# Operand tiles moved to other SBUF bytes, zero-padded scores in block 1, and a PSUM tile copied out by ScalarE where MLA begins

## The chip, the cores and the metric

The kernel runs on one core of a Trainium2 chip. The metric is device time of one execution in microseconds. Three executions of the kernel before took 2668.88, 2670.66 and 2673.24 us (median 2670.66).

## The reference

Two model blocks on 512 tokens of width 1024, all in fp32. Activations are kept transposed (features on partitions, tokens along the free axis).

- **Block 1** puts 16 meta tokens in front (528 columns), then: `h += 0.5*swiglu(rmsnorm(h))` (FFN1, d_ff 2816); a mixer in which sliding-window attention (16 query heads of 64, 4 key heads, sink logits) and an S5 state-space branch are gated and merged through `w_out`; `h += 0.5*swiglu(rmsnorm(h))` again (FFN2, 512 columns), and a final rmsnorm with gain `final_norm`.
- **Block 2** has two layers. Layer 0 mixes with MLA: queries from a rank-512 and keys and values from a rank-256 projection, each with an rms norm, a 64-wide rotary part beside a 128-wide plain part, 16 heads, causal by chunks of 64. Layer 1 mixes with gated linear attention (GLA). After each mixer come layer norm, a conv FFN (`w_up`, a 3-tap conv, gelu gate, `w_down`), layer norm and a gated embedding `x + sigmoid(x W_g + b) * (p W_p)`.

## The kernel before, in words

**Matmuls.** Nearly all products are made by `mm3` (line 173) out of three matmuls of float32r operands: a weight `w` is split into `whi + wlo`, an activation into a high and a low tile (`zh`/`zl`, `mh`/`ml`, `oqh`/`oql` and so on), and `wh*zh`, `wh*zl`, `wl*zh` are summed in one PSUM bank. The stationary operand is a 128x128 piece of the weight, the moving operand the activation tile: 512 columns (`CS`, or `C512`, which is columns 16 to 528 of a 528-column tile), or two pieces of 264 columns (`C528`) where the meta tokens take part. `nat` (line 189) does the same with the activation stationary. Other products (scores, transposes, values, state-space) use plain f32 operands, for which each matmul shows as two in the trace.

**Weights** come by `fetch`: SP issues a 512 KB DMA into `raw`, ScalarE copies it to `whi`, VectorE subtracts for `wlo`.

**Order.** The program is written stage by stage, and a scheduler that simulates a timeline orders each engine's instructions; `issue_after`, `behind` and `chain` hold single instructions back. [...]

**SBUF.** Pools are laid one behind the other and given back in reverse; in a pool, tiles lie in the order of their first use. Of each partition 16384 bytes are reserved at the start (`dynamic_dma_scratch_size` at its default), then 128 bytes of constants, `cp` (21600 bytes), `wp` with the weights (49152), `sm` (960), and `zp` from byte 88224, which is 160 mod 512. `zp` holds `zh0, zl0, zh1, ...`, each in a slot of 2112 bytes (528 columns), so each of the 16 tiles begins 64 bytes later mod 512 than the one before: 160, 224, 288, ... Later stages use the first 512 columns of the same slots. The other operand tiles of 512 columns (2048 bytes) all begin at 416 mod 512 (`yh`, `gh` in pool `m3`; `ov`, `kh` in `a2`; `pth`, `mh`, `ml` in the conv FFNs), at 448 (`oqh`, behind the 16-byte tile `ovr`), or at 480 (`mh`, `ml` of FFN2, pool `f2`). All 128-column pieces of `whi` and `wlo` begin at 224 mod 512.

**Block 1's scores** (`scores1`, line 719): two key heads lie in one 128-row tile `kw`, head `s_` on rows `64*s_` on. For each of 4 query tiles two matmuls of 64 rows are issued, one for each half, into two banks of tag `q` (3 banks), each drained by VectorE with the mask (line 721). There are 8 units (`pp`, `n`) of 4 pairs, and 272 columns of keys (144 for `n == 0`). Between them stand the state-space quarters, queries and gates.

**MLA's beginning**: `project(0)` makes the two plain query products (`pn`) and the rotary product (`pr`) in PSUM, then the norm factor `Rq` of the query tokens (`spread_rsqrt`, into tile `oqR`); `sinT` and `cosT` are multiplied by `Rq` (line 1158, two instructions), and `queries` multiplies `pn` by `Rq` (`qn`) and lets `rotate` (lines 1086 to 1092) read `pr` from PSUM five times on VectorE. Behind the last rotation (`issue_after(last["rot"])`, lines 1238 to 1240) VectorE scales the eight residual tiles `hr` in place. `banks(...)` on line 1241 then deals the eight PSUM banks out anew, and a loop over 64 (head, query block) units follows; `project(1)` is its first filler, its first product in the bank that held `pr`.

Of the kernel before, what the change touches and what calls it, by code (L numbers as in the profile page):

```python
# [53 lines left out]
def body(nc, tc, A, out, es):  # L54
    cp = es.enter_context(tc.tile_pool(name="cp", bufs=1))
    wp = es.enter_context(tc.tile_pool(name="wp", bufs=2))
    sm = es.enter_context(tc.tile_pool(name="sm", bufs=2))
    zp = es.enter_context(tc.tile_pool(name="zp", bufs=1))
    psp = {}
# [47 lines left out]

    woff = {}


# [107 lines left out]
    def split_scaled(src, g, k, n):  # L218
        zh = zp.tile([P, n], F32R, name=f"zh{k}")
        zl = zp.tile([P, n], F32R, name=f"zl{k}")  # L220
        act(zh, src, AF.Copy, scale=g)
        stt(zl, src, g, zh.bitcast(F32), ALU.mult, ALU.subtract)
        return zh, zl

    def sumsq(tiles):
        acc = zp.tile([P, T1], F32, name="acc")
        n = tiles[0].shape[1]
        for k, t in enumerate(tiles):
            if k == 0:
                act(acc[:, :n], t, AF.Square)  # L230
            else:
                sq = zp.tile([P, T1], F32, name="sq", bufs=2)
                act(sq[:, :n], t, AF.Square)
                add(acc[:, :n], acc[:, :n], sq[:, :n], None if k == len(tiles) - 1 else GP)
        return acc[:, :n]
# [28 lines left out]

    def token_rsqrt(acc, scale, eps, R=None):

        pst = token_sums(acc)
        r = rsqrt(pst, pst.shape[1], scale, eps)
        if R is None:
            R = zp.tile([P, T1], F32, name="R")[:, :acc.shape[1]]  # L270
        spread_rsqrt(r, R)
        return r, R
# [353 lines left out]
    hold["dve"] = last["rsqrt"]  # L626
    R = zp.tile([P, T1], F32, name="R")
    hold["act"] = behind(lambda: spread_rsqrt(r, R))
# [19 lines left out]
    with tc.tile_pool(name="m1", bufs=1) as mp:  # L648
        att = mp.tile([P, 8, S], F32, name="att")
        with tc.tile_pool(name="m2", bufs=1) as ap_:  # L650
            for i4 in range(4):
                p = proj(wload("w_in", 1024), P, 0, z, C528)
                uf = ap_.tile([P, 4, MC], F32, name="uf", tag="sc", bufs=3)
                for i in range(2):
                    mul(uf[:, :, i * 66:(i + 1) * 66], p[:, i, :264].rearrange("p (m j) -> p j m", j=4),
                        R[:, i * 264:(i + 1) * 264].rearrange("p (m j) -> p j m", j=4))
                nc.sync.dma_start(u_d[i4 * P:(i4 + 1) * P], uf.rearrange("p j m -> p (j m)"))
            kw = []
            for mo in range(2):
                p = proj(wload("w_in", 1024), P, 0, z, C528)  # L660
                f = ap_.tile([P, T1], F32, name="kf", tag=f"sq{mo}")
                mul(v2(f), p[:, :, :264], v2(R))
                g = ap_.tile([P, 3, 272], F32, name=f"kw{mo}")
                GP.tensor_copy(g[:, 0], f[:, :272])
                for n in range(1, 3):
                    GP.tensor_copy(g[:, n, 0:NM], f[:, 0:NM])
                    GP.tensor_copy(g[:, n, NM:], f[:, NM + n * P:NM + (n + 2) * P])
                kw.append(g)
            banks(b=2, q=3, t=2, o=1)
# [36 lines left out]
            def scores1(u):  # L706
# [7 lines left out]
                for i in range(4):  # L714
                    pq = [pss("q"), pss("q")]
                    for s_ in range(2):
                        r = slice(64 * s_, 64 * s_ + 64)
                        kk = kw[pp][r, max(n - 1, 0), :W]
                        last["sc"] = PE.matmul(pq[s_][:, :W], qf[pp * 4 + i][r, n * P:(n + 1) * P], kk)  # L719
                    for s_ in range(2):  # L720
                        V.tensor_tensor_reduce(sc[s_][:, i, :W], pq[s_][:, :W], mk, 1.0, -3.0e38,
                                               ALU.add, ALU.max, st[s_][0][:, i:i + 1])
# [54 lines left out]
            for ui in range(len(units) + 1):  # L777
# [4 lines left out]
                if ui < 4:  # L782
                    query()
                elif 5 <= ui < 8:
                    gate(zp.tile([P, T1], F32, name="acc" if ui == 5 else "sq", bufs=1 if ui == 5 else 2)[:, :S])
                elif ui == 8:
                    with tc.issue_after(last["sc"].ins):
                        for i in range(2):
                            gate(mp.tile([P, S], F32, name=f"q{i}"))
# [77 lines left out]
    class Norm:  # L867


        def __init__(self, pool, xs, a):  # L870
            self.p, self.xs, self.a = pool, xs, a
            self.aq = zp.tile([P, T1], F32, name="acc")[:, :S]
            self.ad = pool.tile([P, S], F32, name="ad", bufs=1)

        def centre(self):

            pc = pss("s")
            PE.matmul(pc, oness, self.xs[0])
            self.c = zp.tile([P, T1], F32, name="R")[:, :S]
            act(self.c, pc, AF.Copy)  # L880
# [194 lines left out]
    with tc.tile_pool(name="a2", bufs=2) as mp:  # L1075
# [38 lines left out]
        r, _ = token_rsqrt(sumsq(ckv), 1.0 / 256, 1e-5, Rkv)  # L1114
        rkv = mp.tile([P, 4], F32, name="ovr", bufs=1)
        V.tensor_copy(rkv, r)
# [12 lines left out]

        def queries(d, pn, pr):  # L1130
            d["q"], d["r"] = [], []
            for p in pn:
                t = mp.tile([P, S], F32, name="qn", bufs=4)
                mul(t, p, Rq)
                d["q"].append(t)
                yield
            for p in pr:
                qr = mp.tile([P, S], F32, name="qr", bufs=1)
                q2 = mp.tile([P, S], F32, name="q2", bufs=1)
                rotate(qr, q2, p)  # L1140
# [8 lines left out]
        def project(pr_):  # L1149

            d = pair[pr_] = {}
            if pr_ == 0:
                pn = list(nope())
                pst = behind(lambda: token_sums(acc))
                pr = behind(lambda: list(rope()))
                r = rsqrt(pst, 4, 1.0 / 512, 1e-5)
                behind(lambda: spread_rsqrt(r, Rq))
                sc = mul(sinT, sinT, Rq), mul(cosT, cosT, Rq)
            yield from queries(d, pn if pr_ == 0 else nope(), pr if pr_ == 0 else rope())
            w = wload("w_ukv", 1024)  # L1160
# [76 lines left out]
        take([project(0)], 99)  # L1237
        with tc.issue_after(last["rot"].ins):
            for k in range(KD):
                stt(hr[k], hr[k], vcol("final_norm", k), R, ALU.mult, ALU.mult)  # L1240
        banks(b=2, q=2, t=2, o=1, s=1)
# [3 lines left out]
        for i in range(nu + 2):  # L1245
            if i < nu:
# [309 lines left out]
```

## Time and profile before

| | us |
|---|---|
| median of three executions | 2670.66 |
| the profiled execution | 2667.79 |
| its span, first to last instruction | 2666.0 |
| PE busy | 2620.0 (98%) |
| VectorE busy | 1590.7 (60%) |
| ScalarE busy | 959.7 (36%) |
| GpSimd busy | 227.7 (9%) |
| mean granted TensorE clock | 0.991 |

PE is TensorE's matmuls, PEld its weight loads, DVE VectorE, ACT ScalarE, POOL GpSimd. [...]

### The profile page before, as it was taken

The page shows a single profiled execution, that of the slowest core. Times are in us where ns is not written, and L with a number is a line of the kernel's source. Part 1 is how long each engine was busy: PE and PEld are TensorE (multiplying, and loading weights), DVE is VectorE, ACT ScalarE, POOL GpSimd, SP SyncE. Part 2 cuts the span into 40 slices and gives each one's busy share as a digit, 9 for nine tenths or more (in the row PEclk, how much of TensorE's full clock was granted, in tenths as well). Part 3 has the DMA queues.
Part 4 walks back from the last instruction along what each step waited for, and adds up shares of the span by engine and source line. Part 5 has one row for each costly group of instructions (what it writes and reads, how often), then busy time and mean ns, then how long its engine had stood idle before and what let it go on. Part 6 is the DMA issues. An engine that isn't in the chain of part 4 may idle for free.

```text
span 2666.0 us, 35024 instructions
## 1 busy us (share of the span) xinstructions
PE 2620.0 (98%) x13918; PEld 2186.8 (82%) x13918; DVE 1590.7 (60%) x2794; ACT 959.7 (36%) x1483; POOL 227.7 (9%) x186
## 2 busy tenths in 40 slices
PE   8999999899999999999999999999999999999999
PEld 8999999655888888887888878888778777888887
DVE  7985444685556544468766775555663356655556
ACT  4222223243333222234544454333353234433333
POOL 1000001231000000010000110000200011100020
PEclk9999999999999999999999999999999999999999
DMA  5443233331333333322112223333232221433331
GB/s 176 128 131 112 88 95 122 100 91 52 102 95 92 97 99 96 95 91 68 52 56 60 71 79 103 95 95 95 79 98 61 75 72 58 124 95 95 95 90 68
DMA packets 87748, 243.31 MB, mean 91 GB/s; under 512 B 20081, under 2 KB 26097, under 8 KB 87458
## 3 DMA queue, kind: packets, MB, share of 16 engines
q1 hardware_dynamic: 87586, 241.08, 29.3%
q8 instruction: 110, 1.80, 0.3%
q14 instruction: 52, 0.43, 0.0%
HBM read 229.11 MB, written 11.93 MB: 90 GB/s over the span
## 4 chain that ended last, share of the span: by engine, by line
PE 94%; DVE 3%; issue 1%; ACT 1%; DMA 0%; POOL 0%; SPq 0%; DVEq 0%; POOLq 0%; ACTq 0%
PE ps_b L173 63%; PE mm L173 16%; PE ps_b L189 6%; PE ps_o L1228 1%; PE ps_q L1200 1%; PE ps_o L1365 1%; PE ps_t L1216 1%; PE ps_o L772 1%; PE ps_u L1354 1%; PE ps_q L719 1%; PE ps_t L756 0%; DVE h L64 0%; DVE sq L64 0%; DVE wlo L64 0%; PE ps_q L1198 0%
## 5 line engine op out<-in xcount | busy, mean ns | idle before, releaser
L84 ACT ACTIVATE whi<-raw 128x1024 fp32r<-128x1024 f32 (+2 forms) x418 | 432.2, 1036 | 1050.1 <-PE ps_b L173 701.5
L64 DVE TENSOR_TENSOR wlo<-raw,whi 128x1024 fp32r<-128x1024 f32 (+2 forms) x418 | 516.5, 1238 | 341.2 <-ACT whi L84 337.9
L173 PE MATMUL ps_b<-zh,whi 128*128 128x512 f32 (+1 forms) x1656 | 653.1, 395 | 6.5 <-ACT zh L84 2.3
L173 PE MATMUL ps_b<-zh,wlo 128*128 128x512 f32 (+1 forms) x1656 | 654.7, 396 | 0.0
L173 PE MATMUL ps_b<-zl,whi 128*128 128x512 f32 (+1 forms) x1656 | 642.3, 391 | 0.0
L173 PEld LDWEIGHTS ps_b<-zh,whi 128*128 128x128 f32 (+1 forms) x1656 | 310.8, 188 | 82.6 <-issue 4.6
L173 PEld LDWEIGHTS ps_b<-zl,whi 128*128 128x128 f32 (+1 forms) x1656 | 311.3, 188 | 78.3 <-issue 2.6
L173 PEld LDWEIGHTS ps_b<-zh,wlo 128*128 128x128 f32 (+1 forms) x1656 | 310.7, 188 | 69.2
L173 PE MATMUL ps_b<-mh,wlo 128*128 128x512 f32 x528 | 208.5, 395 | 0.0
L173 PE MATMUL ps_b<-ml,whi 128*128 128x512 f32 x528 | 207.7, 393 | 0.0
L173 PE MATMUL ps_b<-mh,whi 128*128 128x512 f32 x528 | 207.6, 393 | 0.0
L173 PE MATMUL mm<-zh,whi 128*128 128x264 f32 x800 | 165.1, 288 | 6.2 <-ACT whi L84 5.8
L173 PE MATMUL mm<-zl,whi 128*128 128x264 f32 x800 | 164.2, 287 | 0.8 <-DVE zl L81 0.8
L173 PE MATMUL mm<-zh,wlo 128*128 128x264 f32 x800 | 164.1, 287 | 0.6 <-DVE wlo L64 0.6
L81 DVE SCALAR_TENSOR_TENSOR cv<-ps_b,vec,cv 128x511 f32<-128x511 f32 (+1 forms) x176 | 130.4, 745 | 16.0 <-ACT cv L84 14.5
L64 DVE TENSOR_TENSOR h<-h,ps_b 128x512 f32<-128x512 f32 x109 | 74.7, 686 | 104.6 <-PE ps_b L173 100.9
L173 PEld LDWEIGHTS mm<-zh,whi 128*128 128x128 f32 x800 | 126.1, 191 | 6.6 <-ACT whi L84 5.8
L173 PEld LDWEIGHTS mm<-zl,whi 128*128 128x128 f32 x800 | 125.2, 191 | 1.5 <-DVE zl L81 1.5
L173 PEld LDWEIGHTS mm<-zh,wlo 128*128 128x128 f32 x800 | 125.6, 190 | 0.8 <-DVE wlo L64 0.8
L64 POOL TENSOR_TENSOR acc<-acc,sq 128x512 f32<-128x512 f32 (+1 forms) x26 | 38.7, 1489 | 948.3 <-ACT sq L84 909.6
L173 PEld LDWEIGHTS ps_b<-mh,whi 128*128 128x128 f32 x528 | 99.2, 188 | 23.2 <-issue 0.5
L173 PEld LDWEIGHTS ps_b<-mh,wlo 128*128 128x128 f32 x528 | 99.2, 188 | 23.1 <-issue 0.5
(421 smaller groups left out, 4001.0 us busy)
## 6 DMA issues: line engine op xcount, KB each, us to landing
raw<-in_ffn_w_dram SPq DMA_DIRECT2D x130, 512.0 KB, 3.5
raw<-in_w_up_dram SPq DMA_DIRECT2D x88, 512.0 KB, 3.6
raw<-in_w_down_dram SPq DMA_DIRECT2D x44, 512.0 KB, 3.6
raw<-in_w_in_dram SPq DMA_DIRECT2D x32, 512.0 KB, 3.5
raw<-in_mla_o_dram SPq DMA_DIRECT2D x16, 512.0 KB, 3.6
raw<-in_ple_g_dram SPq DMA_DIRECT2D x16, 512.0 KB, 3.6
raw<-in_glu_dram SPq DMA_DIRECT2D x8, 512.0 KB, 3.5
raw<-in_w_out_dram SPq DMA_DIRECT2D x8, 512.0 KB, 3.5
```

What stands on the lines that cost most here:

```text
L64: return (e or V).tensor_tensor(o, a, b, op=op)
L81: return V.scalar_tensor_tensor(o, a, s, b, op0=op0, op1=op1)
L84: return SC.activation(o, a, f, **kw)
L173: last["pe"] = PE.matmul(o[:, i, :c1 - c0], lhs, x[k][r][:, c0:c1], start=(k == 0 and j == 0), stop=(k == kt - 1 and j == 2))
L189: PE.matmul(o[:m, :n], x[k][a][:, t0:t0 + m], w[b][:, kk_ * c + m0:kk_ * c + m0 + n], start=(k == 0 and i == 0), stop=(k == kt - 1 and i = ...
L719: last["sc"] = PE.matmul(pq[s_][:, :W], qf[pp * 4 + i][r, n * P:(n + 1) * P], kk)
L772: PE.matmul(po[64 * s_:64 * s_ + 64], vb[n - 1 + j][:, kv * 64:kv * 64 + 64], pT[s_][:, j], start=False, stop=(j == 1))
L1200: PE.matmul(p[:, :N], d["q"][e][:, bs], d["k"][e][:, :N], start=False, stop=True)
L1216: PE.transpose(pt[:, kt * P:(kt + 1) * P], sc[:, kt * P:(kt + 1) * P], ident)
L1228: PE.matmul(po[:, b * P:(b + 1) * P], vt[:, kt, e * P:(e + 1) * P], pT[:, kt * P:(kt + 1) * P], start=(kt == 0), stop=(kt == b))
L1354: PE.matmul(pu[c][:, :256], ek[b][rows, hc], vt[hh][rows, b])
L1365: PE.matmul(po[hh][-1][64 * c:64 * c + 64, (b % 2) * 256:(b % 2) * 256 + 256], qt[hh][:, n * 64:(n + 1) * 64], s_)
```

## The change: what it does

Four things, all on one core and with the same arithmetic:

1. **Bytes.** The reserved region shrinks from 16384 to 2048 bytes (14336 = 28 x 512 less). `zp` gets a 256-byte tile `gap` ahead and slots of 2560 bytes (`zw` = 640 columns), so every `zh`/`zl` of FFN1 and block 1 begins at 160 + 256 = 416 mod 512, and its column 16 at 480. Before `rp` the pool is closed and another, `zq`, opened in its place with a 320-byte `gap`: from FFN2 on every `zh`/`zl` begins at 160 + 320 = 480 mod 512, and, its 20 tiles being of 2048 bytes, so do the pools laid behind it (`a2`, the conv FFNs', GLA's). Gaps of 320 bytes in `m3` and 448 in `rt` put `yh`, `gh` and FFN2's `mh` at 480, and `rkv` takes 512 bytes in place of 16, which puts `oqh` at 480.
2. **Scores of block 1.** Each key head has tiles of its own, `kz[mo][e]`, 128 rows of which the other head's 64 are set to zero by GpSimd; the score matmuls take all 128 rows. Of the copies that fill them those of `e == 1` go to ScalarE, and the 16 meta columns are copied by one broadcast copy each.
3. **MLA's beginning.** ScalarE copies `pr` from PSUM to an SBUF tile `xr` before `spread_rsqrt`, and `rotate` reads `xr`; the two multiplications of `sinT` and `cosT` come behind those of `qn`.
4. **Residual scalings.** The eight scalings of `hr` leave their place behind the rotation; one is issued in each of the units 1 to 8 of the loop.

```diff
+    zpc = tc.tile_pool(name="zp", bufs=1)
+    zp = zpc.__enter__()
+    zp.tile([P, 64], F32, name="gap")
...
+    zw, aw = 640, T1
...
     def split_scaled(src, g, k, n):
-        zh = zp.tile([P, n], F32R, name=f"zh{k}")
-        zl = zp.tile([P, n], F32R, name=f"zl{k}")
+        zh = zp.tile([P, zw], F32R, name=f"zh{k}")[:, :n]
+        zl = zp.tile([P, zw], F32R, name=f"zl{k}")[:, :n]
...
+            kz = [[ap_.tile([P, 3, 272], F32, name=f"kw{mo}{e}") for e in range(2)] for mo in range(2)]
+            for gs in kz:
+                for e, g in enumerate(gs):
+                    GP.memset(g[64 - 64 * e:128 - 64 * e], 0.0)
...
-                g = ap_.tile([P, 3, 272], F32, name=f"kw{mo}")
-                GP.tensor_copy(g[:, 0], f[:, :272])
-                for n in range(1, 3):
-                    GP.tensor_copy(g[:, n, 0:NM], f[:, 0:NM])
-                    GP.tensor_copy(g[:, n, NM:], f[:, NM + n * P:NM + (n + 2) * P])
-                kw.append(g)
+                gs = kz[mo]
+                for e, g in enumerate(gs):
+                    r_ = slice(64 * e, 64 * e + 64)
+                    cpy = (lambda o, i: act(o, i, AF.Copy)) if e else GP.tensor_copy
+                    cpy(g[r_, 0], f[r_, :272])
+                    GP.tensor_copy(g[r_, 1:, 0:NM], f[r_, 0:NM].unsqueeze(1).to_broadcast([64, 2, NM]))
+                    for n in range(1, 3):
+                        cpy(g[r_, n, NM:], f[r_, NM + n * P:NM + (n + 2) * P])
+                kw.append(gs)
...
-                        r = slice(64 * s_, 64 * s_ + 64)
-                        kk = kw[pp][r, max(n - 1, 0), :W]
-                        last["sc"] = PE.matmul(pq[s_][:, :W], qf[pp * 4 + i][r, n * P:(n + 1) * P], kk)
+                        last["sc"] = PE.matmul(pq[s_][:, :W], qf[pp * 4 + i][:, n * P:(n + 1) * P],
+                                               kw[pp][s_][:, max(n - 1, 0), :W])
...
+            gp_.tile([P, 80], F32, name="gap", bufs=1)
...
+    zpc.__exit__(None, None, None)
+    zpc = tc.tile_pool(name="zq", bufs=1)
+    zp = zpc.__enter__()
+    zw, aw = S, S
+    zp.tile([P, 80], F32, name="gap")
...
+        tp.tile([P, 112], F32, name="gap")
...
-        rkv = mp.tile([P, 4], F32, name="ovr", bufs=1)
+        rkv = mp.tile([P, P], F32, name="ovr", bufs=1)[:, :4]
...
-        def queries(d, pn, pr):
+        def queries(d, pn, pr, first=False):
...
+            if first:
+                mul(sinT, sinT, Rq)
+                mul(cosT, cosT, Rq)
             for p in pr:
...
                 r = rsqrt(pst, 4, 1.0 / 512, 1e-5)
+                xr = mp.tile([P, S], F32, name="xr", tag="sc", bufs=4)
+                act(xr, pr[0], AF.Copy)
+                pr = [xr]
                 behind(lambda: spread_rsqrt(r, Rq))
-                sc = mul(sinT, sinT, Rq), mul(cosT, cosT, Rq)
...
         take([project(0)], 99)
-        with tc.issue_after(last["rot"].ins):
-            for k in range(KD):
-                stt(hr[k], hr[k], vcol("final_norm", k), R, ALU.mult, ALU.mult)
...
             take(pq, 1)
+            if 1 <= i <= KD:
+                stt(hr[i - 1], hr[i - 1], vcol("final_norm", i - 1), R, ALU.mult, ALU.mult)
...
-    nc = bacc.Bacc("TRN2", target_bir_lowering=False, num_devices=1)
+    nc = bacc.Bacc("TRN2", target_bir_lowering=False, num_devices=1, dynamic_dma_scratch_size=2048)
```

## Rows read from the trace of the kernel before

**Rows 1.** The page's busy shares, and its chain that ended last, by engine.
```profile
PE 2620.0 (98%) x13918; PEld 2186.8 (82%) x13918; DVE 1590.7 (60%) x2794; ACT 959.7 (36%) x1483; POOL 227.7 (9%) x186
...
PE 94%; DVE 3%; issue 1%; ACT 1%; DMA 0%; POOL 0%; SPq 0%; DVEq 0%; POOLq 0%; ACTq 0%
```
**Rows 2.** Windows over dense stretches: window, length, busy us (x instructions) by engine, clock, DMA.
```profile
96.13:143.02 46.89, 46.89 (x387) 46.89 (x385) 43.21 (x78) 12.78 (x16) 0.00 (x0) 1.00 0.47 136
...
955.95:1000.11 44.16, 44.16 (x193) 36.05 (x192) 18.95 (x22) 12.56 (x16) 0.00 (x0) 1.00 0.30 96
1131.98:1175.51 43.53, 43.53 (x193) 36.04 (x192) 28.98 (x32) 16.12 (x21) 6.68 (x5) 1.00 0.28 88
...
1675.00:1697.39 22.39, 22.39 (x98) 18.05 (x96) 11.64 (x14) 6.08 (x8) 1.29 (x1) 1.00 0.30 94
1697.39:1741.77 44.38, 44.38 (x193) 36.02 (x192) 21.90 (x26) 16.61 (x22) 3.88 (x3) 1.00 0.30 95
...
766.43:811.23 44.80, 44.80 (x194) 35.90 (x193) 22.78 (x27) 17.45 (x25) 10.23 (x6) 1.00 0.31 95
```
**Rows 3.** Groups of matmuls by operands, whole span: count | busy us, mean ns | idle before.
```profile
L173 PE MATMUL ps_b<-zh,whi 128*128 128x512 f32 (+1 forms) x1656 | 653.1, 395 | 6.5 <-ACT zh L84 2.3
...
L173 PE MATMUL ps_b<-mh,wlo 128*128 128x512 f32 x528 | 208.5, 395 | 0.0
...
L173 PE MATMUL ps_b<-gh,wlo 128*128 128x512 f32 x64 | 25.1, 394 | 0.0
```
**Rows 4.** Timeline of PE inside FFN2's up products: start us, us, what.
```profile
965.61 0.40 PE L173 MATMUL ps_b<-zh,whi 128*128 128x512 f32 x1
965.85 0.39 PE L173 MATMUL ps_b<-zl,whi 128*128 128x512 f32 x1
```
**Rows 5.** Timeline of PE where MLA begins; in brackets idle time before, and its releaser.
```profile
1232.59 0.28 PE L189 MATMUL ps_b<-wlo,ovh 128*128 128x256 f32 x1
1237.45 0.69 PE L173 MATMUL ps_b<-oqh,whi 128*128 128x512 f32 x1 [4.59 <-DVE q L64]
1237.94 0.63 PE L173 MATMUL ps_b<-oql,whi 128*128 128x512 f32 x1
```
**Rows 6.** Timeline of DVE over the same stretch.
```profile
1231.41 0.69 DVE L64 TENSOR_TENSOR sinT<-sinT,oqR 128x512 f32<-128x512 f32 x1 [1.08 <-ACT oqR L84]
...
1232.62 1.28 DVE L64 TENSOR_TENSOR qn<-ps_b,oqR 128x512 f32<-128x512 f32 x2
...
1234.52 2.79 DVE L64 TENSOR_TENSOR q<-ps_b,sinT 32x512 f32<-32x512 f32 x4
...
1238.55 5.39 DVE L81 SCALAR_TENSOR_TENSOR h<-h,vec,R 128x512 f32<-128x512 f32 x8
```
**Rows 7.** Timeline of ACT over the same stretch.
```profile
1230.35 0.48 ACT L84 ACTIVATE vt<-ps_b,ovr 128x256 f32<-128x256 f32 x1 [2.69 <-DVE kn L64]
1230.78 0.60 ACT L84 ACTIVATE oqR<-ps_s 128x512 f32<-128x512 f32 x1
```
**Rows 8.** Windows: half clock in MLA's beginning, the first units, and block 1's attention.
```profile
1237.54:1240.95 3.41, 3.41 (x9) 2.64 (x10) 3.41 (x6) 1.26 (x2) 0.00 (x0) 0.50 0.49 154
...
1270.00:1290.00 20.00, 20.00 (x125) 17.04 (x124) 16.64 (x49) 11.32 (x28) 0.00 (x0) 1.00 0.16 53
...
463.00:660.00 197.00, 179.44 (x830) 119.13 (x828) 135.11 (x341) 73.20 (x204) 47.53 (x38) 0.95 0.28 80
```
**Rows 9.** Timeline of PE: a pair of scores, a lone one, and one of MLA's scores.
```profile
588.61 0.73 PE L719 MATMUL ps_q<-kw,q 64*128 64x272 f32 x4
...
590.50 0.72 PE L719 MATMUL ps_q<-kw,q 64*128 64x272 f32 x2
...
1257.57 0.59 PE L1200 MATMUL ps_q<-kn,qn 128*128 128x256 f32 x2
```
**Rows 10.** Timeline of POOL ahead of block 1's attention.
```profile
413.12 0.52 POOL L545 MEMSET M<- 128x512 f32 x1
444.47 0.41 POOL L664 COPY kw<-kf 128x272 f32<-128x272 f32 x1 [30.82 <-DVE kf L64]
```

More of the change, by code (lines that the diff above doesn't have):

```diff
@@ L57, in body @@
     sm = es.enter_context(tc.tile_pool(name="sm", bufs=2))
-    zp = es.enter_context(tc.tile_pool(name="zp", bufs=1))
+    zpc = tc.tile_pool(name="zp", bufs=1)
+    zp = zpc.__enter__()
+    zp.tile([P, 64], F32, name="gap")
     psp = {}
@@ L225, in sumsq @@
     def sumsq(tiles):
-        acc = zp.tile([P, T1], F32, name="acc")
+        acc = zp.tile([P, aw], F32, name="acc")
         n = tiles[0].shape[1]
@@ L231, in sumsq @@
             else:
-                sq = zp.tile([P, T1], F32, name="sq", bufs=2)
+                sq = zp.tile([P, aw], F32, name="sq", bufs=2)
                 act(sq[:, :n], t, AF.Square)
@@ L269, in token_rsqrt @@
         if R is None:
-            R = zp.tile([P, T1], F32, name="R")[:, :acc.shape[1]]
+            R = zp.tile([P, aw], F32, name="R")[:, :acc.shape[1]]
         spread_rsqrt(r, R)
@@ L626, in body @@
     hold["dve"] = last["rsqrt"]
-    R = zp.tile([P, T1], F32, name="R")
+    R = zp.tile([P, aw], F32, name="R")
     hold["act"] = behind(lambda: spread_rsqrt(r, R))
@@ L784, in body @@
                 elif 5 <= ui < 8:
-                    gate(zp.tile([P, T1], F32, name="acc" if ui == 5 else "sq", bufs=1 if ui == 5 else 2)[:, :S])
+                    gate(zp.tile([P, aw], F32, name="acc" if ui == 5 else "sq", bufs=1 if ui == 5 else 2)[:, :S])
                 elif ui == 8:
@@ L871, in __init__ @@
             self.p, self.xs, self.a = pool, xs, a
-            self.aq = zp.tile([P, T1], F32, name="acc")[:, :S]
+            self.aq = zp.tile([P, aw], F32, name="acc")[:, :S]
             self.ad = pool.tile([P, S], F32, name="ad", bufs=1)
@@ L878, in centre @@
             PE.matmul(pc, oness, self.xs[0])
-            self.c = zp.tile([P, T1], F32, name="R")[:, :S]
+            self.c = zp.tile([P, aw], F32, name="R")[:, :S]
             act(self.c, pc, AF.Copy)
@@ L1156, in project @@
                 r = rsqrt(pst, 4, 1.0 / 512, 1e-5)
+                xr = mp.tile([P, S], F32, name="xr", tag="sc", bufs=4)
+                act(xr, pr[0], AF.Copy)
+                pr = [xr]
                 behind(lambda: spread_rsqrt(r, Rq))
-                sc = mul(sinT, sinT, Rq), mul(cosT, cosT, Rq)
-            yield from queries(d, pn if pr_ == 0 else nope(), pr if pr_ == 0 else rope())
+            yield from queries(d, pn if pr_ == 0 else nope(), pr if pr_ == 0 else rope(), pr_ == 0)
             w = wload("w_ukv", 1024)
@@ L1445, in body @@
     dump(hr, S)
+    zpc.__exit__(None, None, None)
     psp["cm"].__exit__(None, None, None)
```

## The prediction

> **What bounds the kernel now.** I read the page's busy shares first: PE is busy 98% of the span, and the chain of waits runs through PE for 94% [rows 1]. VectorE, the next, is at 60%. So an edit on another engine counts only where PE is idle for it, and an edit that makes one PE instruction cheaper counts once per instruction.
>
> Next I read windows over dense stretches, where PE never idles and the clock is full, and divided the length by the number of 512-column matmuls [rows 2]. The reader is to see that the same instruction has several prices:
>
> - FFN2's down products (operands `mh`, `ml` at byte 480): 43.53/192 = 226.7 ns.
> - FFN2's up products (`zh`, `zl`, each tile 64 bytes further): 44.16/192 = 230.0 ns. Inside that stretch the price is not even: the matmul at 965.61 is followed by the next after 0.24 us [rows 4], so the stretch is a mean of cheap and dear ones.
> - the conv FFN's up products (`zh`, `zl` again): 44.38/192 = 231.1 ns.
> - the conv FFN's down products (`mh`, `ml` at 416): 22.39/96 = 233.2 ns.
> - `w_out` in block 1 (`gh` at 416): 44.80/192 = 233.3 ns.
>
> Two stretches at 416 in different blocks agree to 0.1 ns, and the only stretch at 480 is the cheapest, although VectorE has more to do in it (28.98 of 43.53 us) than in conv up (21.90 of 44.38) [rows 2]. The price goes with the byte at which the moving operand begins.
>
> Last I read PE's timeline where it does idle: 4.59 us at MLA's beginning, released by VectorE's rotation [rows 5], and 197.00 - 179.44 = 17.6 us in block 1's attention [rows 8].
>
> **Bytes.** What is counted: 1656 `zh,whi` matmuls [rows 3], times 3 for `zl` and `wlo`: 4968, of which FFN2's up products are 22 x 2 x 8 x 3 = 1056 by the loops. `mh` is 528 x 3 = 1584 [rows 3], of which 528 (22 x 8 x 3) are FFN2's, already at 480; 1056 remain. `gh` is 64 x 3 [rows 3], `yh` the same, `oqh` 288, `ov` and `pth` 96 each: 864. Together 6888 that are not at 480 now and are after.
>
> - FFN2 up: 1056 x (230.0 - 226.7) = 3.4 us.
> - all other `zh`/`zl`: 3912 x (231.1 - 226.7) = 17.2 us.
> - conv down: 1056 x (233.2 - 226.7) = 6.9 us.
> - the 864: priced as `w_out`, 864 x 6.6 = 5.7 us.
>
> Sum 33.2. Two deductions. The conv stretch is 1.1 ns above FFN2's at the same kind of addresses [rows 2], from a cause that I can't see; I let half of it, 0.55 ns, stay on the 5832 matmuls outside FFN2: 3.2 us. And 17.6 of 197 us in block 1's attention are waits [rows 8], where cheaper gates and queries partly lengthen the wait: about 1.5. Left: **-28.5 us**, bounds 0 and -33.
>
> The 264-column products of FFN1 run at 46.89/387 = 121.2 ns [rows 2]; there `zh` moves from mixed bytes to 416 for the first half and 448 for the second. By the 512-column rows the mixed set lies between its neighbours, 2 ns either way for 512 columns, so 1 ns for 264: 2112 x 1 = 2.1 us either way. I take 0.
>
> **MLA's beginning.** PE's last value product starts at 1232.59 and the next product at 1237.45, after 4.59 us of idle time; it needs the bank that the rotation reads [rows 5]. On VectorE `sinT` starts at 1231.41, then `cosT`, then `qn` (1.28 for two), and the four 0.70-us reads of `pr` end at about 1237.3 [rows 6]. Behind the idle time stands a stretch of half clock, 3.41 us with 8 matmuls counted whole [rows 8]: 8 x (0.427 - 0.232) = 1.6 us. So 4.6 + 1.6 = 6.2 us is what can be had.
>
> The copy to `xr` is one 128x512 read of PSUM on ScalarE like `oqR`'s, 0.60 us, and ScalarE idles 2.69 us before 1230.35 [rows 7]; it hides there. If it came behind `oqR` instead it would push `oqR`, and VectorE behind it, by 0.6. The bank is then free at about 1228 to 1232, so the rotation no longer matters to PE. Next in line is VectorE's `qn`: it now comes first, 1.28 us from 1231.4, and frees the banks of the plain products at 1232.7, when PE is just through with the values. PE has then two further products of `project(1)` (24 matmuls, 5.5 us) before it needs a bank that VectorE has still to free by the next `qn`; VectorE must first do `sinT`, `cosT` (1.3) and the rotation (about 4). I keep 1.2 us of wait there: 6.2 - 1.2 = **-5 us**, bounds 0 and -6.2.
>
> The eight scalings of `hr` take 5.39 us behind the rotation [rows 6]. Spread over units 1 to 8 they are 0.67 us in each; in such units VectorE is busy 16.64 of 20 us [rows 8], 3.4 free for some seven units' 4.7. While PE stays full there it costs nothing; were none of it hidden it would be 5.4 us, and a unit's wait for VectorE is the sign. I take 0, and fold the loss into the range.
>
> **Scores of block 1.** 64 score matmuls, 32 pairs. One pair on two row halves takes 0.73 us for four records, that is, the two run side by side; a lone one takes 0.72 for two records [rows 9]. About half of the pairs stand as pairs in the timeline. With 128 rows two can't share the array. The nearest 128-row f32 matmul, MLA's 256 columns, takes 0.59 [rows 9], so 0.62 for 272. In stream cost, a pair goes from 0.73 to about 1.08: 16 x 0.35 = +5.6; lone ones get no dearer and, by 0.72 to 0.62, cheaper: 32 x 0.10 = -3.2. Net +2.4, partly inside the 17.6 us of waits: **+1 us**, bounds -4 and +8. The mean clock of that stage is 0.95, about a tenth of it at half level [rows 8]; full rows may raise or lower that, and I take 0.
>
> [...]
>
> The four half-tile clears on GpSimd resemble its 128x512 memset, 0.52 us, and the first key copy comes after 30.82 us of idle time there [rows 10]; 0, at worst 4 x 0.8 = 3.3. Moving the `e == 1` copies to ScalarE is 6 instructions like 0.41 [rows 10], with tens of us before the first score: 0.
>
> **Sum.** -28.5 - 5 + 1 = -32.5. The profiled execution took 2667.79: span 2666.0 and 1.8 around it. 2667.8 - 32.5 = 2635.3. The median of the runs is 2.9 above the profiled one, so 2638.
>
> **The rivals.**
>
> *Only one kind of tile gains.* If the price of the `zh`/`zl` stretches comes from something other than where each tile begins (the alternation of `zh` and `zl`, say), they stay at 231 and only the 1920 others gain, 1920 x 6.55 = 12.6. For: conv up is 1.1 above FFN2 up at like addresses [rows 2]. Against: the uneven steps inside the stretch [rows 4]. Time: 2670.7 - 12.6 - 5 + 1 = 2654.
>
> *The byte does nothing, or the tiles don't land there.* FFN2's 226.7 would then come from lighter traffic of other engines; or the unread `gap` tiles take no room and all lands at 160 mod 512. Against the first: VectorE and GpSimd have more to do in FFN2's window than in conv up's [rows 2]. Sum -5 + 1 = -4: 2667, within 0.2%.
>
> [...]
>
> *Slower: one dear byte for all.* Today a `zh`/`zl` stretch mixes dear steps such as 0.24 with cheaper ones [rows 4]. If for these tiles 480 is the dear place (FFN2's `mh` being cheap for its own reason), all 6888 go to 235 at least, the least that rounds to 0.24; the mean now is (1056 x 230.0 + 3912 x 231.1 + 1920 x 233.25)/6888 = 231.5. 6888 x 3.5 = +24, less 4: 2691. It decides from a mean of 232.1 after the change, where the gain of 4 is eaten up.
>
> **How the numbers follow.** Forecast .80, only one kind .10, byte does nothing .06, dear byte .04. The forecast's own range is 2626 to 2649: -33 of bytes with all of MLA's and the scores at -4, to half of MLA's, scores at +8 and the 0.55 doubled. The range to give takes in most of the first rival too: 2623 to 2658. What a measurement of this kernel can tell from no change is 0.2%, 5.3 us. Faster by more: forecast and first rival, .90; within: .06; slower: .04.
>
> **What would show it.** Right: windows of 192 `zh`/`zl` matmuls of conv up of 43.5 to 43.8 us, conv down of 96 at 21.8 (2 of 32 us come from each 0.3 ns); no idle time of 4 us before `project(1)`'s first product, and no half clock behind it; the 16 score pairs at 0.62 twice. Wrong: conv up still at 44.4 (first rival), conv down still at 22.4 (second), either above 44.8 per 192 (third); new waits for VectorE in the units 1 to 8, or more half clock in block 1's attention.

## The result, and the profile after

The changed kernel took 2636.02 us (median of 4; 2631.25 to 2638.03) against 2671.36 us before: a ratio of 0.9866 with a 95% interval of 0.9849 to 0.9883, or -35.3 us. In two more comparisons it gave 0.9863 [0.9847, 0.9880] and 0.9884 [0.9868, 0.9901]. The prediction was 2638.

The page's busy shares and the chain by engine, as in [rows 1]:

```profile
PE 2586.8 (98%) x13918; PEld 2191.2 (83%) x13918; DVE 1586.1 (60%) x2794; ACT 961.8 (37%) x1490; POOL 232.7 (9%) x190
...
PE 93%; DVE 4%; issue 1%; ACT 1%; DMA 0%; POOL 0%; SPq 0%; DVEq 0%; POOLq 0%; ACTq 0%
```

The same 13918 matmuls keep PE busy for 33.2 us less, and the span falls by 32.5 (2666.0 to 2633.5): PE was the bound and still is.

The windows of [rows 2] on the changed kernel, in the order of time: FFN1's up products, `w_out`, FFN2 up, FFN2 down, conv down, conv up. Columns: length, then busy us (x instructions) of PE, PEld, DVE, ACT, POOL, then clock, DMA share, GB/s. A matmul's record overlaps the next one's, 395 ns long on the mean [rows 3] and followed by the next start after 0.24 us [rows 4], so in a dense stretch the price of one is the length divided by their number. At a granted clock of 0.50, half clock, 8 matmuls counted whole took 3.41 us [rows 8], 0.43 each, where at 1.00 they cost 0.227 to 0.233 [rows 2].

```profile
95.43:141.52 46.09, 46.09 (x387) 46.09 (x386) 43.15 (x78) 12.87 (x16) 0.00 (x0) 1.00 0.46 135
758.71:802.23 43.52, 43.52 (x193) 36.04 (x192) 22.97 (x27) 17.45 (x25) 10.23 (x6) 1.00 0.32 97
945.09:988.61 43.52, 43.52 (x193) 36.05 (x192) 18.95 (x22) 12.54 (x16) 0.00 (x0) 1.00 0.32 97
1119.17:1162.69 43.52, 43.52 (x193) 36.05 (x192) 26.77 (x33) 17.51 (x24) 8.45 (x6) 1.00 0.33 97
1654.73:1676.49 21.76, 21.76 (x97) 18.02 (x96) 11.60 (x14) 6.18 (x8) 1.30 (x1) 1.00 0.32 98
1676.49:1720.01 43.52, 43.52 (x193) 36.05 (x192) 21.89 (x26) 16.60 (x22) 3.87 (x3) 1.00 0.32 97
```

Five stretches that cost 226.7 to 233.3 ns per matmul now cost 43.52/192 = 226.7 each, whatever VectorE, ScalarE and GpSimd do meanwhile. FFN1's 264-column products fell too, 46.89 to 46.09 us for 384.

Where the 32.5 us of the span came from, between matmuls that both traces have (all in us; the last column is the time at half clock, before and after):

| stretch | before | after | change | half clock |
|---|---|---|---|---|
| start to block 1's first score | 486.7 | 481.9 | -4.9 | 3.4, then 0 |
| to the first product behind block 1's last score | 152.2 | 151.8 | -0.5 | 20.5, then 13.7 |
| to the first `oqh` product | 577.5 | 569.4 | -8.2 | 0, 0 |
| to MLA's unit 24 (the 25th) | 103.7 | 100.1 | -3.7 | 3.4, then 0 |
| to the first conv down product | 299.2 | 297.3 | -2.0 | 6.8, 6.8 |
| to GLA's first state product | 414.4 | 408.3 | -6.2 | 6.8, then 10.2 |
| to the second conv FFN's first down product | 270.2 | 270.9 | +0.7 | 3.4, then 6.8 |
| to the end | 361.9 | 354.0 | -7.9 | 5.1, then 3.9 |

MLA's beginning on PE, where [rows 5] had one idle time of 4.59 us (every idle time from 1219 to 1237 is shown; then DVE and ACT, as [rows 6, 7]):

```profile
1220.49 0.50 PE L176 MATMUL ps_b<-oqh,whi 128*128 128x512 f32 x1 [0.97 <-ACT vt L86]
...
1233.12 0.50 PE L176 MATMUL ps_b<-ovh,whi 128*128 128x512 f32 x1 [1.67 <-DVE q L66]
...
1235.10 0.39 PE L192 MATMUL ps_b<-whi,ovh 128*128 128x256 f32 x1 [0.34 <-DVE kn L66]
```
```profile
1218.05 1.29 DVE L66 TENSOR_TENSOR qn<-ps_b,oqR 128x512 f32<-128x512 f32 x2 [1.08 <-ACT oqR L86]
1219.25 0.68 DVE L66 TENSOR_TENSOR sinT<-sinT,oqR 128x512 f32<-128x512 f32 x1
...
1221.17 2.77 DVE L66 TENSOR_TENSOR q<-xr,sinT 32x512 f32<-32x512 f32 x4
```
```profile
1214.29 0.58 ACT L86 ACTIVATE xr<-ps_b 128x512 f32<-128x512 f32 x1
...
1217.42 0.60 ACT L86 ACTIVATE oqR<-ps_s 128x512 f32<-128x512 f32 x1
```

The copy stands in ScalarE's idle time, as forecast, and does not delay `oqR`. The reader is to see that the one wait became three, 2.98 us together. There is no half clock behind them (3.41 us before).

Block 1's scores, a lone one and two groups of two, as [rows 9]:

```profile
582.34 0.62 PE L728 MATMUL ps_q<-kw,q 128*128 128x272 f32 x2
583.90 1.18 PE L728 MATMUL ps_q<-kw,q 128*128 128x272 f32 x4
585.37 1.08 PE L728 MATMUL ps_q<-kw,q 128*128 128x272 f32 x4
```

At full clock the lone ones of 272 columns take 0.62 to 0.73 us, where those of 64 rows took 0.62 to 0.72.

### The profile page after: what moved, and what is told of

Read it like the earlier page. It is cut to its first block, busy times and chain, and to the rows that moved or that the text cites. A ratio compares the mean times of both kernels' runs of the same rounds, so it can differ in the third digit from the quotient of the medians.

```text
span 2633.5 us, 35043 instructions
## 1 busy us (share of the span) xinstructions
PE 2586.8 (98%) x13918; PEld 2191.2 (83%) x13918; DVE 1586.1 (60%) x2794; ACT 961.8 (37%) x1490; POOL 232.7 (9%) x190
## 4 chain that ended last, share of the span: by engine, by line
PE 93%; DVE 4%; issue 1%; ACT 1%; DMA 0%; POOL 0%; SPq 0%; DVEq 0%; POOLq 0%; ACTq 0%
PE ps_b L176 61%; PE mm L176 15%; PE ps_b L192 6%; PE ps_o L1252 1%; PE ps_q L1224 1%; PE ps_o L1388 1%; DVE wlo L66 1%; PE ps_t L1240 1%; PE ps_o L782 1%; PE ps_u L1377 1%; PE ps_q L728 1%; DVE h L66 0%; DVE sq L66 0%; PE ps_t L766 0%; PE ps_q L1222 0%
## 5 line engine op out<-in xcount | busy, mean ns | idle before, releaser
L176 PE MATMUL ps_b<-zh,wlo 128*128 128x512 f32 (+1 forms) x1656 | 643.6, 389 | 0.0
L83 DVE SCALAR_TENSOR_TENSOR cv<-ps_b,vec,cv 128x511 f32<-128x511 f32 (+1 forms) x176 | 130.4, 744 | 15.1 <-ACT cv L86 13.7
```

The lines of the kernel that those rows point to most:

```text
L83: return V.scalar_tensor_tensor(o, a, s, b, op0=op0, op1=op1)
L176: last["pe"] = PE.matmul(o[:, i, :c1 - c0], lhs, x[k][r][:, c0:c1], start=(k == 0 and j == 0), stop=(k == kt - 1 and j == 2))
```

## The experiments

Each kernel is the one before or the changed one with the edit named. Theory P of the first two is the prediction's.

### The placement alone, and all the rest without it

The first kernel has the hunks of part 1 of the change, the second those of parts 2 to 4 and `dynamic_dma_scratch_size=2048`.

Expected of the placement alone: 

> The kernel before with the byte placement alone (first part of the change: smaller reserve, gaps, wider slots). Theory P (the price of a matmul goes with the byte of its moving operand, and that is nearly the whole gain): windows of 192 conv up matmuls at 43.5 us, conv down of 96 at 21.8, w_out 192 at 43.5; whole -29 to -31 us, ratio 0.988 to 0.989. Rival Q (the rest carries a good part of the -35): -20 us or less, ratio above 0.992. MLA's beginning keeps its 4.6 us of idle time and block 1's score pairs their 0.73 us in either.

Expected of the rest: 

> The change without the byte placement: 128-row scores, rotary copy and residual scalings on the kernel before (only the reserved region is cut, by a multiple of 512, so every operand tile begins at the byte mod 512 where it began before). Theory P: conv up 44.4, conv down 22.4 as before; MLA's beginning -3 us (idle 4.6 to about 3, half clock gone), scores between -1 and +3; whole 0 to -4 us, ratio 0.998 to 1.000. Rival Q: -10 us or more, ratio under 0.996.

Measured: 2640.04 us, ratio 0.9892 [0.9877, 0.9907], for the placement; 2663.44, ratio 0.9971 [0.9958, 0.9983], for the rest. Conv down and conv up of each:

```profile
1659.90:1681.66 21.76, 21.76 (x98) 18.02 (x96) 11.61 (x14) 6.18 (x8) 1.30 (x1) 1.00 0.32 97
1681.66:1725.18 43.52, 43.52 (x194) 36.04 (x192) 21.89 (x26) 16.60 (x22) 3.87 (x3) 1.00 0.31 97
```
```profile
1675.52:1697.91 22.39, 22.39 (x97) 18.05 (x96) 11.64 (x14) 6.10 (x8) 1.30 (x1) 1.00 0.31 94
1697.91:1742.29 44.38, 44.38 (x193) 36.03 (x192) 21.90 (x26) 16.61 (x22) 3.87 (x3) 1.00 0.29 95
```

The placement is worth -29 us (2669.06 x 0.0108), and the prices go with it to the hundredth. The rest is worth -8 by the ratio (2669.06 x 0.0029) and -5.6 by the medians, more than expected: theory P gave at most -4. The second kernel's mean granted clock was 0.993 to 0.995 in its runs, where the kernel before had 0.990 or 0.991, and the surplus goes with that. Its profile, of the slowest of its executions, is 3.0 us shorter than that of the kernel before, inside what theory P gave: -3.4 up to MLA's unit 24, +2.9 in the stretch of block 1's scores with 20.5 us of half clock in both, and -3.4 in the last two stretches of the table, which have 7.8 us less of half clock. In which stage the faster executions gain the remainder is not shown.

### What of the placement makes the price

All weight tiles lie at 224 mod 256, and 480 is 224 mod 256 too. So the prediction's rule (the price goes with the byte at which the moving operand begins) could not be told from another: that it goes with the distance between the moving and the stationary operand. Two kernels tell them apart: one with the weights moved, and one with matmuls alone.

```diff
 # weights 64 bytes further, operands where they were
     cp = es.enter_context(tc.tile_pool(name="cp", bufs=1))
+    cp.tile([P, 16], F32, name="pad")
...
-    zp.tile([P, 64], F32, name="gap")
+    zp.tile([P, 48], F32, name="gap")
...
-    zp.tile([P, 80], F32, name="gap")
+    zp.tile([P, 64], F32, name="gap")
```

Expected with the weights moved: 

> The changed kernel with every weight tile (whi, wlo, raw) 64 bytes further, from 224 to 288 mod 512 (32 mod 256), the operand tiles left at 480 by gaps that are 64 bytes smaller. Theory A: conv up 43.5 us per 192, conv down 21.8 per 96, whole as the changed kernel, 2636. Rival B: conv up 44.7, conv down 22.4, whole about 40 us longer, 2675.

The matmuls alone, with `w` and `m` from 0 to 7:

```python
for i in range(24):
    a = (i % 4) * P + 8 * w
    b = (i % 4) * 512 + 8 * m
    nc.tensor.matmul(o[:, :n], W[:, a:a + P], M[:, b:b + n], start=(i == 0), stop=(i == 23))
```

Expected of them: 

> A kernel that computes nothing of the reference: after a warm-up, 192 blocks of 24 float32r matmuls (512, then 264, then 256 columns), with the stationary operand at each of 8 bytes mod 256 (0, 32, ... 224: second letter A to H of the output's name) and the moving operand at each of the same 8 (first letter A to H), all other engines still. Theory A (the moving operand's own byte counts): 512 columns cost 226.8 ns with the moving operand at 224 whatever the stationary one's, and 232 to 233 at 32, 96, 160 and 192. Rival B (how the two lie to each other counts; all stationary tiles of the kernel lie at 224): 226.8 on the diagonal where the two bytes are equal, 232 or more off it. Rival C (other engines' traffic makes the difference): one price for all 64 blocks.

Measured with the weights moved: 2675.76 us, where the rival gave 2675. Conv down and conv up:

```profile
1679.20:1701.60 22.40, 22.40 (x97) 18.05 (x96) 11.65 (x14) 6.10 (x8) 1.30 (x1) 1.00 0.29 95
1701.60:1746.40 44.80, 44.80 (x193) 36.10 (x192) 21.89 (x26) 16.62 (x22) 3.85 (x3) 1.00 0.31 94
```

The operands still lie at 480, and cost 233.3 ns, what `gh` at 416 did [rows 2]. The kernel of matmuls alone, in windows over blocks of 24 (no DVE column: it does nothing). Moving and stationary byte mod 256 are, line by line, 32 and 32; 96 and 96; 224 and 224; 96 and 32; 224 and 32; 0 and 96; 0 and 224; and for 256 columns 160 and 224; 96 and 160:

```profile
69.41:74.87 5.46, 5.46 (x25) 4.51 (x24) 0.00 (x0) 0.00 (x0) 1.00 0.00 0
169.80:175.25 5.45, 5.45 (x26) 4.50 (x24) 0.00 (x0) 0.00 (x0) 1.00 0.00 0
370.40:375.87 5.47, 5.47 (x25) 4.50 (x24) 0.00 (x0) 0.00 (x0) 1.00 0.00 0
80.48:85.98 5.50, 5.50 (x25) 4.51 (x24) 0.00 (x0) 0.00 (x0) 1.00 0.00 0
102.81:108.41 5.60, 5.60 (x25) 4.49 (x24) 0.00 (x0) 0.00 (x0) 1.00 0.00 0
153.00:158.62 5.62, 5.62 (x25) 4.52 (x24) 0.00 (x0) 0.00 (x0) 1.00 0.00 0
331.28:336.88 5.60, 5.60 (x25) 4.50 (x24) 0.00 (x0) 0.00 (x0) 1.00 0.00 0
...
735.56:738.32 2.76, 2.76 (x27) 2.76 (x26) 0.00 (x0) 0.00 (x0) 1.00 0.00 0
684.53:687.26 2.73, 2.73 (x26) 2.73 (x25) 0.00 (x0) 0.00 (x0) 1.00 0.00 0
```

The windows of 512 columns give 5.45 to 5.47 us (227 to 228 ns) where the two bytes are equal, at 32 as well as at 224; 5.60 to 5.62 (233 to 234 ns) at a distance, with 64 between (5.50, 229 ns). No DMA and no other engine runs, so traffic is out. From start to start of matmuls inside a block, in ns, by distance of the moving operand behind the stationary one (mod 256), over the blocks with the stationary byte at 32:

| distance | 0 | 32 | 64 | 96 | 128 | 160 | 192 | 224 |
|---|---|---|---|---|---|---|---|---|
| 512 columns | 227.7 | 233.4 | 229.3 | 233.9 | 233.5 | 234.0 | 233.5 | 233.0 |
| 264 columns | 121.7 | 121.8 | 120.9 | 121.4 | 123.5 | 121.8 | 121.3 | 120.1 |
| 256 columns | 119.7 | 118.0 | 118.0 | 119.6 | 118.7 | 117.4 | 113.7 | 118.3 |

Most entries recur within 2 ns for the other seven stationary bytes; where the moving byte lies under the stationary one, some of the two narrower shapes stray by up to 5. At 256 columns and a distance of 192 that concerns the blocks with the stationary byte at 64, 96 and 192, which take 117.7 to 117.8; the other five take 113.7 to 114.8. For 512 columns the distance decides, not the byte; for 256 it is not the whole of it, and they want another distance than 512. The period is 256 bytes and not 512: by the layout, operands and weights of the changed kernel lie 256 bytes apart mod 512, in the blocks at distance 0 they lie at the same byte mod 512, and both are cheap (226.7, and 227 to 228 ns).

The table also comes near the mixed prices of the kernel before: its `zh` tiles lay by turns at distances of 192 and 64 from the weights, its `zl` tiles at 0 and 128, which makes 231 ns on the mean. The conv FFN's up products had 231.1, FFN2's 230.0 [rows 2]; where the 1.1 between them comes from stays open.

A last kernel closes it: weights and operands both 64 bytes further.

```diff
     cp = es.enter_context(tc.tile_pool(name="cp", bufs=1))
+    cp.tile([P, 16], F32, name="pad")
```

Expected: 

> The changed kernel with weights and operand tiles all 64 bytes further, so that both begin at 32 mod 256 (the weights from 224 to 288 mod 512, zh, zl and the others from 480 to 544). Theory B (the distance between the two bytes counts): conv up 43.5 us per 192 and conv down 21.8 per 96, the whole as the changed kernel, 2632 to 2638. Theory A (the moving operand's own byte): 32 is a dear byte, conv up 44.5 or more, whole 2665 or more.

Measured: 2626.74 us in one run, under the 2632 to 2638 expected: it had 26.1 us of half clock (mean clock 0.995), the three profiles of the changed kernel 37.1 to 50.4. Both stretches are back at 226.7 ns with every operand at 32 mod 256:

```profile
1652.41:1674.17 21.76, 21.76 (x98) 18.02 (x96) 11.61 (x14) 6.18 (x8) 1.30 (x1) 1.00 0.30 97
1674.17:1717.69 43.52, 43.52 (x194) 36.04 (x192) 21.89 (x26) 16.63 (x22) 3.87 (x3) 1.00 0.31 97
```

Theory A, the prediction's own rule, has fallen: byte 32, 229 ns with the stationary operand at 224 in the kernel of matmuls alone, gives 226.7 with the weights at 32.

### The scores of block 1

The changed kernel once more, the changed kernel with scores of 64 rows, and the kernel before with scores of 128 rows alone. The second kernel has these lines, and the key tiles, clears and copies of the kernel before with them; the third has part 2 of the change on the kernel before:

```diff
-                        last["sc"] = PE.matmul(pq[s_][:, :W], qf[pp * 4 + i][:, n * P:(n + 1) * P],
-                                               kw[pp][s_][:, max(n - 1, 0), :W])
+                        r = slice(64 * s_, 64 * s_ + 64)
+                        kk = kw[pp][r, max(n - 1, 0), :W]
+                        last["sc"] = PE.matmul(pq[s_][:, :W], qf[pp * 4 + i][r, n * P:(n + 1) * P], kk)
...
```

Expected of the changed kernel: 

> The changed kernel once more, to stand beside x6 on the same chip: 2633 to 2638 us, ratio 0.986 to 0.988 by either theory.

Expected with 64 rows: 

> The changed kernel with block 1's scores of 64 rows as before; placement, rotary copy and residual scalings stay. Theory S (the 128-row scores cost what they cost in stream time: the stage was 2.9 us longer in x2 at equal half-clock time): 3 us faster than x5, 2632. Rival C (full rows keep the clock up: the stage's half-clock time was 27.3 us in x1 with 64 rows and 13.7 in the changed kernel): half-clock time in block 1's attention back to 20 to 27 us, mean clock 0.003 lower, and the kernel 1 to 5 us slower than x5, 2637 to 2640.

Expected of 128 rows alone: 

> The kernel before with the 128-row scores alone (and the smaller reserve, a multiple of 512). Theory S: a pair of adjacent scores 0.66 to 0.92 us, a lone one 0.65 to 0.56, score group's busy time 29.1 to 33.2 us, the stage from the first score on 152.2 to about 155 at 20.5 us of half clock. Rival C: the same prices, but half-clock time in the stage under 15 us, and the stage no longer than 152.5.

Measured: 2632.64 us (2632.43 to 2634.54) with 128 rows, 2637.68 (2635.71 to 2642.71) with 64, on the same chip: the edit gains 5 us there, though the ratios' intervals overlap (0.9863 [0.9847, 0.9880] and 0.9883 [0.9868, 0.9897]). Alone on the kernel before, 2664.62 in one run. The score group with 64 rows and with 128 (count | busy us, mean ns | idle before), from these last two kernels:

```profile
L722 PE MATMUL ps_q<-kw,q 64*128 64x272 f32 (+1 forms) x128 | 29.5, 413 | 0.5 <-DVE at L724 0.3
```
```profile
L725 PE MATMUL ps_q<-kw,q 128*128 128x272 f32 (+1 forms) x128 | 33.3, 382 | 0.1
```

The 128 rows cost 4 us more of PE. Now the attention stage, as in the last line of [rows 8]: changed kernel, its second profile, with 64 rows, with 128 rows alone, and the changed kernel's third profile.

```profile
458.70:654.60 195.90, 177.14 (x829) 124.96 (x828) 135.28 (x341) 72.97 (x204) 47.41 (x38) 0.97 0.28 80
```
```profile
458.80:654.60 195.80, 177.19 (x829) 124.93 (x828) 135.24 (x341) 72.97 (x203) 47.44 (x38) 0.97 0.27 80
```
```profile
458.80:660.50 201.70, 183.63 (x830) 123.11 (x828) 135.37 (x341) 73.10 (x203) 46.60 (x38) 0.92 0.27 78
```
```profile
464.00:659.50 195.50, 176.39 (x826) 123.18 (x825) 135.35 (x341) 73.05 (x204) 47.46 (x38) 0.97 0.27 80
```
```profile
458.50:658.50 200.00, 181.22 (x829) 127.12 (x827) 135.27 (x341) 72.84 (x203) 47.42 (x38) 0.94 0.26 79
```

The difference goes with the granted clock: 0.97 against 0.92. Over all profiles here, the stage spent 20.5 to 30.7 us at half clock with 64 rows (5 profiles, mean 25.9) and 10.2 to 23.9 with 128 (8 profiles, mean 14.5). The price in PE time is theory S's, the sum is rival C's. But the groups overlap: one profile of the changed kernel had 23.9, and in that comparison the kernel had 2636.02. So the gain is one of the mean. As an estimate from these rows: 11.4 us less of half clock, at which a matmul takes about twice as long (8 in 3.41 us in [rows 8]), are 5.7 us, less the 2.9 by which the stage is longer at equal half clock (the kernel with all but the placement against the kernel before), so some 3 us on the mean; no run shows that sum by itself. What in the 64-row scores goes with the lower clock was not isolated: key tiles, clears and copies change together with the rows.

### The copy and the scalings, each alone

Expected of the copy alone (the kernel before with part 3): 

> The kernel before with the rotary copy and the later scaling of the tables alone; the eight residual scalings stay behind the rotation on VectorE. Theory M (the copy frees the bank, but the scalings then stand between the rotation and what PE needs next): the 4.6 us of idle time before project(1) fall to about 1, and a second wait of 5 to 7 us comes up before PE's key products (1.7 in the changed kernel): first unit no earlier than 28 us after the first query product (28.2 before, 27.2 after). Rival N (the scalings are in nobody's way): first unit after 27 us as in the changed kernel.

Expected of the scalings alone (part 4): 

> The kernel before with the eight residual scalings alone moved into units 1 to 8; rotation and PSUM as before. Theory M (the idle time belongs to the rotation's reads, the scalings only delay what follows): the 4.6 us of idle time before project(1) stay, first unit about 28 us after the first query product, units 0 to 24 1 to 2.5 us shorter than before's 75.5; whole -1 to -3 us. Rival N (the scalings cost what they take wherever they stand): units 0 to 24 as long as before or longer, whole no faster.

Measured: 2677.38 and 2669.00 us, one run each, with 2668 to 2669 for the kernel before on those chips. PE's idle times and the DVE instructions that matter, with the copy alone:

```profile
1239.23 0.49 PE L173 MATMUL ps_b<-oqh,whi 128*128 128x512 f32 x1 [0.97 <-ACT vt L84]
...
1250.60 0.79 PE L173 MATMUL ps_b<-ovh,whi 128*128 128x512 f32 x1 [2.70 <-DVE qn L64]
...
1257.83 0.80 PE L173 MATMUL ps_b<-ovh,whi 128*128 128x512 f32 x1 [2.92 <-DVE q L64]
```
```profile
1244.55 5.39 DVE L81 SCALAR_TENSOR_TENSOR h<-h,vec,R 128x512 f32<-128x512 f32 x8
1249.85 0.69 DVE L64 TENSOR_TENSOR qn<-ps_b,oqR 128x512 f32<-128x512 f32 x1
```

And with the scalings alone:

```profile
1241.08 0.47 PE L173 MATMUL ps_b<-oqh,whi 128*128 128x512 f32 x1 [4.58 <-DVE q L64]
```

Theory M's waits came in both. Alone, the copy only moves the wait: the eight scalings now stand between the rotation and the `qn` whose bank PE wants, and the waits come to 6.59 us where 4.59 stood. The first unit comes 31.4 us after the first query product, against 27.4 in the kernel with all but the placement. The 28.2 of the kernel before do not compare: with the copy 130 matmuls stand ahead of the first unit, without it 112. A like measure is the way to unit 24 (537 matmuls with the copy alone, 543 in the others): 105.9 us with the copy alone, 103.7 before, so the copy alone loses 2.2 us, 6.8 us of half clock (3.4 before) included. Alone, the scalings leave the 4.58 and gain 1.0 us in units 0 to 24, the lower end of what theory M gave; the whole, forecast 1 to 3 us faster, was not (2669.00, before 2668.07 in the median), so one run leaves rival N's second half open: its profile has 3.1 us more in the stretch of block 1's scores, at 23.9 us of half clock against 20.5. Together the two edits gain 3.4 us up to unit 24 in the kernel without the placement (103.7 to 100.4): 1.5 less of idle time, and 3.4 us of half clock less, which by the estimate above is worth some 1.7. Of the 9.6 us by which the span with the copy alone is longer than that of the kernel before, 4.8 lie in block 1's attention at 27.3 us of half clock, which this edit does not touch.

### A step further: another distance for 256 columns

By the table, block 1's values and GLA's keys, values and gates (1080 matmuls with 256 columns of weight moving, not the 1056 of the expectation) want a distance of 192. Each weight slot gets 256 bytes more; weights of those products start at column 0 of it, all others at column 16; `raw` gets 224 bytes more and the gaps 64, so that all other distances stay.

```diff
+        nv = name in ("gla_k", "gla_v", "gla_r") or (name == "w_in" and off // (P * n) in (6, 7))
+        s_ = 0 if nv else 16
-        hi = wp.tile([P, 1024], F32R, tag="whi", name="whi", bufs=5)
...
+        hi = wp.tile([P, 1088], F32R, tag="whi", name="whi", bufs=5)[:, s_:s_ + 1024]
...
```

Expected: 

> The changed kernel, with the weights of block 1's values and of GLA's keys, values and gates (256-column moving operands, activation stationary) 64 bytes ahead of all other weights, so that the moving operand begins 192 bytes mod 256 behind the stationary one where now both begin at 480. By the table of x3 (113.7 to 114.8 ns at a distance of 192, 119.7 at 0; theory B of the distance): 1056 matmuls at about 114 in place of 119.5, -5.5 us, ratio 0.002 under that of x11. Rival G (these stages are held by something else, or the clock gives it back): 118 to 120 ns, or half-clock time 4 us or more up in GLA, and no faster than x11.

Expected of the changed kernel beside it: 

> The changed kernel beside x10 on the same chip: 2632 to 2638 us, ratio 0.986 to 0.988 by either theory.

Measured: 2628.91 us, ratio 0.9851 [0.9836, 0.9866], beside 2636.02, ratio 0.9884 [0.9868, 0.9901]. The runs don't overlap (2626.05 to 2629.84 against 2635.02 to 2640.44). Block 1's values, 120 matmuls: the kernel before, the changed one, and this one.

```profile
450.41:464.45 14.04, 14.04 (x120) 13.59 (x121) 2.19 (x4) 3.09 (x6) 2.29 (x5) 1.00 0.13 39
```
```profile
445.84:460.09 14.25, 14.25 (x120) 13.79 (x121) 2.17 (x4) 4.13 (x10) 2.36 (x5) 1.00 0.14 38
```
```profile
445.55:459.16 13.61, 13.61 (x121) 13.15 (x122) 2.09 (x4) 4.15 (x10) 2.36 (x5) 1.00 0.14 40
```

Here lies a loss that the change brought unseen: its placement made these products dearer, 14.04 to 14.25. The mean from start to start of all of them where PE is dense is 117.8 ns before, 119.4 changed, 114.6 here; 1080 x 4.8 = 5.2 us. The price came as theory B of the distance has it, and this version beats both kernels. Not all of the 7.1 us between the two medians is the price: of the 9.8 us between the two profiles, 4.6 lie in the stretches in which these products stand, and 5.4 in the stretch of block 1's scores, which had 13.7 us of half clock here and 23.9 in the changed kernel.

## Why the prediction was right, point by point

- **PE's price per matmul, -28.5 forecast.** The placement alone gave -29. The 512-column terms came out as worked out: 226.7 ns in all dense stretches shown, so the 0.55 ns kept back for the conv FFNs (3.2 us) was not needed. Two terms were missed. The 264-column products, taken at 0 with 2.1 us either way, gained 2400 x (122.1 - 120.0) = 5.0 us (46.89 to 46.09 for 384; there are 2400, not the 2112 of the up products alone; and the prediction's 121.2 divides by 387, three of which only overlap the window). And the 256-column products, of which the prediction says nothing, lost 1080 x 1.6 = 1.7 us. These roughly cancel against the clock: the profile of the placement alone had 64.1 us of half clock where the kernel before had 51.5.
- **The mechanism of it was wrong.** "The price goes with the byte at which the moving operand begins" is not so: with the weights moved the same byte is dear (233.3 ns at 480), and with both moved another byte is as cheap (226.7 at 32 mod 256). What counts for 512 columns is the distance to the stationary operand (227.7 ns at 0, 229.3 at 64, 233.0 to 234.0 at the others of the table), which the kernel before can't show, since all its weights lie at one byte. The forecast held because the change left the weights where they were; that its rule and the right one agree there is luck.
- **The rivals.** "Only one kind of tile gains" and "the byte does nothing" fell by the windows at 226.7. "One dear byte" had its answer too: there is no dear byte, only a dear distance, and with every tile at one the kernel with the weights moved took 2676, where the rival was priced at 2691. Traffic of other engines is out by the matmuls alone too: with every other engine still, the same 24 matmuls took 5.45 or 5.62 us, by where PE's own two operands lie.
- **MLA's beginning, -5 forecast, about -3.4 measured.** The copy, its cover and the half clock came as said. The remaining wait was put at 1.2 us and is 2.98, in three pieces, the first of which (0.97, for ScalarE's `vt`) was not foreseen. That the scalings cost nothing in the units is right (with the scalings alone PE has no idle time over 0.15 us in units 0 to 23), but the prediction treats them as a side edit: without their move the copy loses time.
- **The scores, +1 forecast.** The 1.08 for two stands on no row and was the author's estimate; the runs showed 1.08 to 1.18, where two of 64 rows ran side by side in 0.73. But the busy time rose by 4.2 us (29.1 to 33.3) where +2.4 was worked out, for two reasons in the count: in the kernel before only 16 of the 64 scores stand alone and 48 in groups of two to five, where the prediction took 32 and 32; and the lone ones did not get 0.10 cheaper, 0.69 to 0.66 on the mean of those of 272 columns. The term "I take 0" for the clock was mis-sized: half clock in the stage fell from 20.5 to 13.7 us in the profiles compared, on the mean of all by 11. So the stage came out 0.5 us shorter, not longer; at equal half clock it was 2.9 longer. That +1 lies so near the measured -0.5 is luck: two errors of some 2 and 3 us cancel. GpSimd's four clears took 3.23 us before the first score and nobody waited, as forecast.
- **The sum.** -28.5 - 5 + 1 = -32.5 against a span that is 32.5 shorter and a median that is 35.3 shorter. The parts that were off (+1.6 for MLA, a few us of clock, -5.0 and +1.7 of unpriced matmuls, 3.2 held back) happen to cancel within that. The changed kernel's twelve executions lie between 2631.25 and 2640.44 us, so the agreement of the last microsecond proves nothing. The forecast's own range, 2626 to 2649, comes out some 2 us higher at both ends by its terms from the median of 2670.7.

## What to carry to other kernels

When a dense stretch of one instruction has different prices in different places, divide lengths by counts and look for what differs in the operands; then ask what was constant in all of them, because a rule read from the trace can hide it (here the weights' byte). Before laying tiles out, measure the price of each matmul shape over the distance mod 256 between its two operands: a kernel of 0.75 ms gave the whole table, and 256 columns were cheapest at another (113.7 ns at 192) than 512 (227.7 at 0). And an edit that removes a wait should be looked at with the work queued behind the waiter: up to the same point of the work the copy alone lost 2.2 us, the scalings alone gained 0.9, and the pair gained 3.4.

## What the runs showed of the hardware

- The time of a float32r matmul of 512 columns went with the distance mod 256 between the starting bytes of its moving and its stationary operand: 226.7 to 228 ns at 0, about 229 at 64, 232 to 234 at the other multiples of 32. At 256 columns 192 was the cheapest in five of eight blocks (113.7 to 114.8 ns; 117.7 to 117.8 in the other three) and 0 was dear (119.7 to 120.1). What makes the difference was not found out.
- Two f32 matmuls of 64 rows on the two row halves ran side by side in 0.73 us, where the two of 128 rows took 1.08 to 1.18; yet the stage with 64-row scores got a lower granted clock in most profiles (0.92 to 0.95 against 0.94 to 0.97).
- The difference between executions of one kernel went with the granted clock: the changed kernel's runs of 2631.25, 2635.32 and 2638.03 us had mean clocks of 0.994, 0.992 and 0.991, some 2 us for each 0.001.
